# One task for the products with v, and output bias and LayerNorm vectors loaded per group, in a two-layer decoder trunk

## The chip, the cores and the metric

One Trainium2 chip, one of its cores. The metric is the time of the program on the device in microseconds (us); the smaller, the better.

## What is computed

Two layers (DEPTH = 2) run over 2048 rows of 1024 values, all in 32-bit floats. Each layer is one projection into nine pieces, two mixers, a gated sum of the two, an output product and a LayerNorm after the residual sum:

```
h = x @ w_in + b_in                      # q k v z_a u_g v_g z_g g_a g_g
y_a = sliding_window_attention(q, k, v, sinks) * silu(z_a)        # 8 query heads, 2 kv heads, window 128
y_g = spatial_gating(gelu(u_g), gelu(v_g), ...) * silu(z_g)       # LayerNorm(v_g), mixing within chunks of 128 rows
merged = sigmoid(g_a) * (y_a @ w_branch_attn) + sigmoid(g_g) * (y_g @ w_branch_gmlp)
out = merged @ w_out + b_out
x = layer_norm(ALPHA * x + out, ln_g, ln_b)
```

The last two lines use the three vectors of length 1024 that the change is about: `b_out`, `ln_g`, `ln_b`.

## The kernel before

**Groups and units.** Each layer runs over four groups of 512 rows; (l, g) names group g of layer l, so that the order is (0,0), (0,1) ... (1,3). A group works through 54 weight units in order: k, v, four for q, four wide ones for v_g, twelve for z_a, z_g and u_g, sixteen for the gates, eight for the two branch products, and eight (46 to 53) for the output product. A unit is 24 matmuls of 128 x 512 on TensorE (PE), since each product of 32-bit values is made from a high and a low half in three products (`accum_t`, `accum_w`; all of these matmuls are recorded at L178).

**Weights.** In group 0 of a layer a raw unit of 512 KB is loaded to `wr`, split into halves by ScalarE (ACT, L137) and VectorE (DVE, L138), and both halves are stored as `kept` (1 MB). Groups 1 to 3 load the kept halves instead (`w<-kept`, 1 MB, L129). `next_unit` issues the load three or four units ahead. SyncE (SP) issues these loads, those of x and those of the residual, in one queue and in order.

**Side tasks.** Attention, the LayerNorm of v_g, the mixing and the preparing of the next group's x are small tasks in a list (`side`). `mm` calls `step`, which takes a task off the list at a set pace; a scheduler then fixes one order for each engine, and each engine keeps to it. The products with v are `pv_task` (L446): 32 matmuls for each head pair into one bank of PSUM (the accumulators' memory), then a product with `sza` on DVE (L452). In group 0 of a layer there is one task for each pair; in the other six groups there are two, of two pairs each, `pv_task(0, 1)` in the midst of the transposes of the probabilities and `pv_task(2, 3)` after the tasks that normalise v_g.

**The next x.** In groups (0,3), (1,0), (1,1) and (1,2) the next group's x is read from memory, where the LayerNorm left it (`x_later`): eight tiles of 128 x 512, each turned by 16 STREAM_TRANSPOSE instructions on DVE (L291). Those of the first five tiles run in the gate units; those of the last three, 48 instructions, and the splits of these tiles (L203, tiles x) come at the end of the group.

**End of a group.** Eight tiles `y` of residual are loaded (L605) and turned to ALPHA*y + bias on DVE by eight SCALAR_TENSOR_TENSOR (L699). The output product has two halves of 512 columns (h = 0, 1) with four units each; within a unit PE goes over the four row blocks b = 0 to 3, six matmuls each, into four of the five PSUM banks of the pool `MM`. After a half DVE adds each bank to its y (L686) and takes statistics (L688); this is what sets a bank free. The first matmul of h = 1 goes to the fifth bank; that for b = 1 has to wait for the bank that L686 of b = 0, h = 0 empties. The LayerNorm then runs as side tasks in the next group, by ACT (L676) and GpSimd (POOL, L677 and the line behind it).

**The three vectors.** `bo_b`, `lg_b` and `lb_b` are constant tiles of 128 x 1024, each filled by one broadcast DMA of 512 KB from POOL's queue (`out_consts`, L257 to L259), once for each layer: in the first units of (0,0) and around the start of layer 1.

**Temporaries.** `TT` takes a tile of 128 x 512 from the pool `tp`, which has 15.

Of the kernel before, what the change touches and what calls it, by code (L numbers as in the profile page):

```python
# [8 lines left out]
F32 = mybir.dt.float32  # L9
F32R = mybir.dt.float32r  # L10
AF = mybir.ActivationFunctionType
ALU = mybir.AluOpType
PSUM = bass.MemoryType.PSUM

P = 128
# [23 lines left out]
Q_DELAY = 20  # L39
P_DELAY = 10  # L40
LAG = 5
LAG2 = 3
NEARLY = 5


# [5 lines left out]
def trunk_kernel(ctx, tc, xg, xt, wu, bcol, bvg, sinks, lngc, lnb, wsp, bsp, bout, ln_g, ln_b,  # L51
# [4 lines left out]
    def sb(name, bufs):  # L56
        return ctx.enter_context(tc.tile_pool(name=name, bufs=bufs))
# [2 lines left out]
    xp = sb("xp", 2 * KC)  # L60
    yp = sb("yp", 16)
    mp = sb("mp", 16)
    tp = sb("tp", 15)
    wr = sb("wr", 2)
    wp = sb("wp", 4)
    small = sb("small", 3)
# [19 lines left out]
    def TT(shape=None):  # L86
        return tp.tile(shape or [P, T], F32, name=nm("t"), tag="t")
# [4 lines left out]
    def AT(shape=None):  # L92
        return ps_at.tile(shape or [P, T], F32, name=nm("at"), tag="at")

    def S(shape, tag):
        return small.tile(shape, F32, name=nm(tag), tag=tag)
# [119 lines left out]
    vg_b = const.tile([P, GW], F32, name="vg_b")  # L216
    wsT = const.tile([P, NGR, P], F32, name="wsT")
    bias2 = const.tile([P, NGR, P], F32, name="bias2")
    bo_b = const.tile([P, D], F32, name="bo_b")
    lg_b = const.tile([P, D], F32, name="lg_b")  # L220
    lb_b = const.tile([P, D], F32, name="lb_b")
    kept = [[dram.tile([P, 2, 1024], F32, name=f"kept{l}_{n}") for n in range(NUNITS)] for l in range(DEPTH)]
    x1 = [dram.tile([P, NB, D], F32, name=f"x1_{i}") for i in range(NG)]

# [28 lines left out]
                              in0=ps.rearrange("p g t -> p (g t)"), in1=t2, op=ALU.add)  # L253
        return always, go

    def out_consts(l):
        pool.dma_start(out=bo_b, in_=bout[l].partition_broadcast(P))  # L257
        pool.dma_start(out=lg_b, in_=ln_g[l].partition_broadcast(P))
        pool.dma_start(out=lb_b, in_=ln_b[l].partition_broadcast(P))  # L259


    def x_first(g):
# [46 lines left out]
    def group(l, g, xs):  # L309
# [44 lines left out]
            sp.dma_start(out=b8, in_=score_bias)  # L354
            pool.dma_start(out=vg_b, in_=bvg[l].partition_broadcast(P))

        if g == 0 and l > 0:
            out_consts(l)

        sza, szg = [], []  # L360


# [75 lines left out]

        def pv_task(*cs):
            def go():  # L440
                pos = {c: AT() for c in cs}
                for c in cs:
                    for b in range(NB):
                        for kb in range(2):
                            for j in range(2):
                                pe.matmul(pos[c][j * HD:(j + 1) * HD, b * P:(b + 1) * P],  # L446
                                          lhsT=VT[:, b + kb, j * HD:(j + 1) * HD],
                                          rhs=att[c]["p"][b // 2][1 - kb][:, 2 * (b % 2) + j, :],
                                          start=kb == 0, stop=kb == 1, skip_group_check=True)
                for c in cs:  # L450
                    y = TT()
                    dve.tensor_tensor(out=y, in0=pos[c], in1=sza[c], op=ALU.mult)  # L452
                    ys[c] = hilo(Y, y)
                    del att[c]
            return (lambda: count[0] >= due["p", cs[-1], 1]), go
# [28 lines left out]
        for c in range(NPAIR):  # L484
            for hf in range(2):
                for r in range(4):
                    side.append(t_task(c, hf, r))
                    if two and c == 2 and hf * 4 + r == LAG2:
                        side.append(pv_task(0, 1))
                    if not two and c and hf * 4 + r == LAG:  # L490
                        side.append(pv_task(c - 1))
        pace[0] = PACE_T
# [47 lines left out]

        uz = set()
        side.extend([v_stats(b) for b in range(NB)] + [nop] + [v_norm(b) for b in range(NB)])
        side.append(pv_task(2, 3) if two else pv_task(3))
        side.extend(mix_task(gi) for gi in range(NGR))
        for i in range(4):
            ps = item()
# [18 lines left out]
        for c in range(KC):  # L565
            if c == 3 and nl == DEPTH - 1:
                nxt, early, late = x_later(ng)
                pace[0] = PACE_E
                side.extend(early)
            ga = gate(BGA + c)  # L570
            uz.add(4 + c)
            gs[c] = ga, gate(BGG + c)
            if c % 2 == 0:
                continue
            if c == 1:
                flush()
                if l + 1 < DEPTH and g == NG - 1:
                    side.append(mix_consts(l + 1))
                elif l == 0 and g == 0:
                    out_consts(0)  # L580
            for cc in (c - 1, c):
                W = next_unit(P)
                sa, sg = gs.pop(cc)
                pa = MM()
                accum_t(pa, W, 0, ys[0:4])
                dve.tensor_tensor(out=sa, in0=sa, in1=pa, op=ALU.mult)  # L586
                pg = MM()
                accum_t(pg, W, 4, ys[4:8])
                dve.tensor_tensor(out=sg, in0=sg, in1=pg, op=ALU.mult)  # L589
                pool.tensor_tensor(out=sa, in0=sa, in1=sg, op=ALU.add)  # L590
                ms.append(hilo(M, sa))
# [9 lines left out]
        for b in range(NB):  # L601
            for h in range(2):
                row = g * NB + b
                src = xt[row * P:(row + 1) * P] if l == 0 else x1[g][:, b, :]
                sp.dma_start(out=rt[b][h], in_=src[:, h * T:(h + 1) * T])  # L605
        st = S([P, NB, 2, 6], "st2")
        mv = S([P, NB, 2], "mv2")
        rs = S([P, NB, 1], "rs2")
# [21 lines left out]
                               in1=mhalf[:, 0:n].unsqueeze(2), op=ALU.pow)  # L630

        def part(b, h):
            r, hs = rt[b][h], slice(h * T, (h + 1) * T)
            dve.scalar_tensor_tensor(out=r, in0=r, scalar=mv[:, b, 0:1], in1=lg_b[:, hs],
                                     op0=ALU.subtract, op1=ALU.mult)

        def norm(b):
            row = g * NB + b
            dst = out[row * P:(row + 1) * P] if l == DEPTH - 1 else x1[g][:, b, :]
            if last and b == NB - 1:  # L640
                for h in range(2):
                    r, hs = rt[b][h], slice(h * T, (h + 1) * T)
                    if h:
                        part(b, h)
                    dve.scalar_tensor_tensor(out=r, in0=r, scalar=rs[:, b, :], in1=lb_b[:, hs],
                                             op0=ALU.mult, op1=ALU.add)
                    sp.dma_start(out=dst[:, hs], in_=r)
                return
            if last:

                nmr = S([P, 1], "nmr")
                dve.scalar_tensor_tensor(out=nmr, in0=mv[:, b, 0:1], scalar=-1.0, in1=rs[:, b, :],
                                         op0=ALU.mult, op1=ALU.mult)
                own = [(T, D)] if b < NB - 2 else [(0, T), (T, T + 256)]
                rest = (0, T) if b < NB - 2 else (T + 256, D)

                def at(lo, hi):
                    return rt[b][lo // T][:, lo % T:(hi - 1) % T + 1], slice(lo, hi)
                for lo, hi in own:
                    r, cs = at(lo, hi)  # L660
                    dve.scalar_tensor_tensor(out=r, in0=r, scalar=mv[:, b, 0:1], in1=lg_b[:, cs],
                                             op0=ALU.subtract, op1=ALU.mult)
                for lo, hi in own:
                    r, cs = at(lo, hi)
                    dve.scalar_tensor_tensor(out=r, in0=r, scalar=rs[:, b, :], in1=lb_b[:, cs],
                                             op0=ALU.mult, op1=ALU.add)
                r, cs = at(*rest)
                act.activation(out=r, in_=r, func=AF.Identity, bias=nmr, scale=rs[:, b, :])
                pool.tensor_tensor(out=r, in0=r, in1=lg_b[:, cs], op=ALU.mult)
                pool.tensor_tensor(out=r, in0=r, in1=lb_b[:, cs], op=ALU.add)  # L670
                for h in range(2):
                    sp.dma_start(out=dst[:, h * T:(h + 1) * T], in_=rt[b][h])
                return
            for h in range(2):
                r, hs = rt[b][h], slice(h * T, (h + 1) * T)
                act.activation(out=r, in_=r, func=AF.Identity, bias=nm4[:, b, :], scale=rs[:, b, :])  # L676
                pool.tensor_tensor(out=r, in0=r, in1=lg_b[:, hs], op=ALU.mult)  # L677
                pool.tensor_tensor(out=r, in0=r, in1=lb_b[:, hs], op=ALU.add)
                pool.dma_start(out=dst[:, hs], in_=r)

        for h in range(2):
# [12 lines left out]
            for u in range(1 if tail else 4):  # L694
                W = next_unit(T)
                for b in range(NB):
                    accum_w(banks[b], W, ms, u, b)
                    if u == 0:
                        dve.scalar_tensor_tensor(out=rt[b][h], in0=rt[b][h], scalar=ALPHA,  # L699
                                                 in1=bo_b[:, h * T:(h + 1) * T], op0=ALU.mult, op1=ALU.add)  # L700
            if tail:
                Ws = [next_unit(T) for _ in range(3)]
                for b in range(NB):
# [123 lines left out]
```

## Time and profile before

| | us |
|---|---|
| median of 3 runs (2541.79 to 2543.31) | 2541.99 |
| the profiled execution, own time | 2541.27 |
| its span from first to last instruction | 2539.6 |
| PE busy (99% of the span) | 2515.7 |
| DVE busy (57%) | 1438.2 |
| ACT busy (27%) | 692.3 |
| POOL busy (17%) | 427.4 |

The mean granted TensorE clock over the span is 0.998 of its full speed. A timeline has one row for a run of like instructions: start, length, engine, line, operation and tiles, their count, and in brackets the idle time of the engine just before and what ended it. A DMA row ends with the time from issue to landing.

### The profile page before, as it was taken

To read this page: it belongs to the slowest core of one execution; us is meant where nothing else is said; L and a number is where in the kernel's file an instruction comes from. 1 tells how busy PE (TensorE), PEld (TensorE's weight loads), DVE (VectorE), ACT (ScalarE), POOL (GpSimd) and SP (SyncE) were. 2 spreads that over 40 slices of the span, in tenths; PEclk is the share of its full clock that TensorE was granted. 3 is DMA by queue.
4 is the path that set the end of the run, shared out by engine and by line. 5 is a ranking of instruction groups with operands and counts; after the bars stand their busy time and mean duration, and the time that the engine had idled before them with its cause. 6 is when DMAs were issued, how large, how long until landed. Compare 5 with 4: busy or idle time off the path is not lost.

```text
span 2539.6 us, 32405 instructions
## 1 busy us (share of the span) xinstructions
PE 2515.7 (99%) x12176; PEld 2093.2 (82%) x12176; DVE 1438.2 (57%) x3755; ACT 692.3 (27%) x1323; POOL 427.4 (17%) x446
## 2 busy tenths in 40 slices
PE   8999999999999999999999999999999999999998
PEld 6888888888888888888878888888888888888886
DVE  7963568213682137825689577772567724676215
ACT  4433333211431114211154322421115211151110
POOL 1120041100411004210041100420004200032001
PEclk9999999999999999999999999999999999999999
DMA  9788964457554576556776897655665556655454
GB/s 320 252 294 299 325 247 177 167 198 260 205 182 166 198 253 212 181 182 221 252 276 232 293 324 281 220 183 173 224 220 207 181 185 211 225 201 182 176 188 180
DMA packets 116108, 568.39 MB, mean 224 GB/s; under 512 B 12112, under 2 KB 28528, under 8 KB 60528
## 3 DMA queue, kind: packets, MB, share of 16 engines
q1 hardware_dynamic: 109776, 546.35, 61.1%
q0 software_dynamic: 6176, 19.97, 2.1%
q8 instruction: 96, 1.57, 0.2%
q14 instruction: 60, 0.49, 0.1%
HBM read 436.25 MB, written 130.02 MB: 223 GB/s over the span
## 4 chain that ended last, share of the span: by engine, by line
PE 93%; DVE 3%; issue 2%; DMA 1%; ACT 0%; POOL 0%; SPq 0%; DVEq 0%; ACTq 0%; POOLq 0%
PE mm L178 87%; PE at L377 2%; PE at L446 2%; PE at L529 1%; DVE t L291 1%; DMA wr<-in_wu 1%; DVE w L138 0%; DVE y L699 0%; ACT y L676 0%; SPq L267 0%; DVE x L203 0%; POOL rs L629 0%; DVE vt L350 0%; ACT w L137 0%; DVE t L589 0%
## 5 line engine op out<-in xcount | busy, mean ns | idle before, releaser
L178 PE MATMUL mm<-x,w 128*128 128x512 f32 x6528 | 1515.8, 391 | 9.5 <-ACT x L202 7.1
L178 PEld LDWEIGHTS mm<-x,w 128*128 128x128 f32 x6528 | 1220.6, 188 | 265.7 <-ACT x L202 7.6
L178 PE MATMUL mm<-y,w 128*128 128x512 f32 x1536 | 353.6, 389 | 0.0
L178 PE MATMUL mm<-w,m 128*128 128x512 f32 x1536 | 349.8, 389 | 0.2 <-DVE y L686 0.2
L178 PEld LDWEIGHTS mm<-w,m 128*128 128x128 f32 x1536 | 288.3, 188 | 60.4 <-DVE y L686 0.6
L178 PEld LDWEIGHTS mm<-y,w 128*128 128x128 f32 x1536 | 288.3, 188 | 59.8
L427 DVE STREAM_TRANSPOSE t<-t 32x128 f32<-32x128 f32 x1024 | 309.2, 302 | 14.1
L590 POOL TENSOR_TENSOR t<-t,t 128x512 f32<-128x512 f32 x64 | 84.0, 1312 | 1011.3 <-DVE t L589 953.8
L138 DVE TENSOR_TENSOR w<-wr,w 128x1024 fp32r<-128x1024 f32 x108 | 147.7, 1368 | 140.1 <-ACT w L137 139.2
L586 DVE TENSOR_TENSOR t<-t,mm 128x512 f32<-128x512 f32 x64 | 43.7, 683 | 293.0 <-PE mm L178 292.9
L558 ACT ACTIVATE t<-mm,bcol 128x512 f32<-128x512 f32 x128 | 88.2, 689 | 423.2 <-PE mm L178 423.1
L178 PE MATMUL mm<-w,x 128*128 128x512 f32 x768 | 190.7, 392 | 0.0
L291 DVE STREAM_TRANSPOSE t<-t 32x128 f32<-32x128 f32 x512 | 154.9, 303 | 50.7 <-DMA t<-x 43.5
L137 ACT CAST w<-wr 128x1024 fp32r<-128x1024 f32 x108 | 113.1, 1047 | 206.1 <-DMA wr<-in_wu 91.9
L178 PEld LDWEIGHTS mm<-w,x 128*128 128x128 f32 x768 | 139.1, 189 | 25.5
L432 POOL TENSOR_SCALAR_AFFINE_SELECT t<-t 128x512 f32<-128x512 f32 x64 | 44.7, 699 | 572.2 <-DVE t L427 538.2
L202 ACT CAST m<-t 128x512 fp32r<-128x512 f32 x64 | 39.8, 621 | 288.1 <-POOL t L590 288.0
L409 ACT ACTIVATE t<-t,negm 128x128 f32<-128x128 f32 x256 | 99.3, 389 | 55.8 <-DVE negm L399 55.4
L686 DVE TENSOR_TENSOR y<-y,mm 128x512 f32<-128x512 f32 x64 | 43.9, 687 | 119.2 <-PE mm L178 119.2
L385 DVE CUSTOM_DVE_ANT_0 t<-at,b 128x256 f32<-128x256 f32 (+1 forms) x256 | 97.0, 412 | 17.0 <-PE at L377 14.6
L452 DVE TENSOR_TENSOR t<-at,m 128x512 f32<-128x512 f32 x32 | 22.0, 686 | 124.2 <-PE at L446 124.2
L676 ACT ACTIVATE y<-y,nm,rs 128x512 f32<-128x512 f32 x56 | 41.1, 805 | 182.8 <-DVE nm L717 182.6
(104 smaller groups left out, 1780.8 us busy)
## 6 DMA issues: line engine op xcount, KB each, us to landing
w<-kept SPq DMA_DIRECT2D x324, 1024.0 KB, 4.8
kept<-w SPq DMA_DIRECT2D x108, 1024.0 KB, 4.9
wr<-in_wu SPq DMA_DIRECT2D x108, 512.0 KB, 5.9
t<-in_xg SPq DMA_DIRECT2D x32, 256.0 KB, 6.6
y<-in_xt SPq DMA_DIRECT2D x32, 256.0 KB, 6.4
x<-y POOLq DMA_DIRECT2D x32, 256.0 KB, 5.2
t<-x SPq DMA_DIRECT2D x32, 256.0 KB, 5.6
y<-x SPq DMA_DIRECT2D x32, 256.0 KB, 6.3
```

The source lines that it names most:

```text
L137: act.copy(out=t[:, 0, :], in_=r)
L138: dve.tensor_tensor(out=t[:, 1, :], in0=r, in1=f(t)[:, 0, :], op=ALU.subtract)
L178: pe.matmul(o, lhsT=a, rhs=b, start=start, stop=stop, skip_group_check=skip)
L291: dve.transpose(out=outs[k][32 * i:32 * i + 32, :, 32 * r:32 * r + 32], in_=tiles[k][32 * r:32 * r + 32, :, 32 * i:32 * i + 32])
L377: pe.matmul(ps[:, j, :], lhsT=q[c][j][:, b * P:(b + 1) * P], rhs=KT[a][j][:, b * P:b * P + 2 * P], start=a == 0, stop=a == 1)
L385: dve.tensor_tensor_reduce(out=t[:, j, lo:], in0=ps[:, j, lo:], in1=b8[:, 2 * c + j, lo:], scale=1.0, scalar=NEG, op0=ALU.add, op1=ALU.max ...
L409: act.activation(out=w, in_=w, func=AF.Exp, bias=negm[:, bb, j:j + 1], scale=HD ** -0.5, accum_out=sums[:, bb, j:j + 1])
L427: dve.transpose(out=cur_[32 * i:32 * i + 32, :, 32 * r:32 * r + 32], in_=w[32 * r:32 * r + 32, :, 32 * i:32 * i + 32])
L432: pool.affine_select(out=prev_, in_=cur_, pattern=[[0, 4], [-1, P]], compare_op=ALU.is_gt, fill=0.0, base=0, channel_multiplier=1)
L446: pe.matmul(pos[c][j * HD:(j + 1) * HD, b * P:(b + 1) * P], lhsT=VT[:, b + kb, j * HD:(j + 1) * HD], rhs=att[c]["p"][b // 2][1 - kb][:, 2 ...
L558: act.activation(out=t, in_=ps, func=AF.Sigmoid, bias=bias(i))
L590: pool.tensor_tensor(out=sa, in0=sa, in1=sg, op=ALU.add)
```

## The change

`pv_task` takes all four pairs at once in the six groups with g > 0, at the place where pairs 2 and 3 were; its fourth bank comes from the pool `MM`. The constant tiles for the three vectors are gone. Instead `out_consts(l, src)` takes two tiles of 128 x 512 from the temporaries and fills them by two DMAs of 256 KB each from SP's queue; it is called three times in each group, behind the loads of the residual. That is six broadcasts for a group and 48 in all, where six of 512 KB ran in the whole program. The pool of temporaries grows from 15 to 21.

```diff
-    tp = sb("tp", 15)
+    tp = sb("tp", 21)
...
-    bo_b = const.tile([P, D], F32, name="bo_b")
-    lg_b = const.tile([P, D], F32, name="lg_b")
-    lb_b = const.tile([P, D], F32, name="lb_b")
...
-    def out_consts(l):
-        pool.dma_start(out=bo_b, in_=bout[l].partition_broadcast(P))
-        pool.dma_start(out=lg_b, in_=ln_g[l].partition_broadcast(P))
-        pool.dma_start(out=lb_b, in_=ln_b[l].partition_broadcast(P))
+    def out_consts(l, src):
+        ts = [TT() for _ in range(2)]
+        for h in range(2):
+            sp.dma_start(out=ts[h], in_=src[l][h * T:(h + 1) * T].partition_broadcast(P))
+        return ts
...
-        if g == 0 and l > 0:
-            out_consts(l)
...
-                pos = {c: AT() for c in cs}
+                pos = {c: AT() if i < 3 else MM() for i, c in enumerate(cs)}
...
-                    if two and c == 2 and hf * 4 + r == LAG2:
-                        side.append(pv_task(0, 1))
...
-        side.append(pv_task(2, 3) if two else pv_task(3))
+        side.append(pv_task(0, 1, 2, 3) if two else pv_task(3))
...
-                elif l == 0 and g == 0:
-                    out_consts(0)
...
                 sp.dma_start(out=rt[b][h], in_=src[:, h * T:(h + 1) * T])
+        bo_b, lg_b, lb_b = (out_consts(l, src) for src in (bout, ln_g, ln_b))
...
                     if u == 0:
                         dve.scalar_tensor_tensor(out=rt[b][h], in0=rt[b][h], scalar=ALPHA,
-                                                 in1=bo_b[:, h * T:(h + 1) * T], op0=ALU.mult, op1=ALU.add)
+                                                 in1=bo_b[h], op0=ALU.mult, op1=ALU.add)
```

The other uses of the three vectors (LayerNorm) read the new tiles in the same way.

The change moves instructions in two places that matter below. The first is DVE's order at the end of group (0,3). There `t<-t` STREAM_TRANSPOSE are the turns of the next x, `y<-y,bo_b` (after: `y<-y,t`) is ALPHA*y + bias, `t<-t,mm` and `m<-t,m` belong to the last branch products, and `y<-y,mm` empties a bank. Before, the stretch in which the transposes lie and the first three of ALPHA*y + bias:

```order
L291 STREAM_TRANSPOSE t_9798<-t_9342 32x4x32 x14
L586 TENSOR_TENSOR t_9542<-t_9542,mm_9633 128x512
L291 STREAM_TRANSPOSE t_9798<-t_9342 32x4x32 x2
L291 STREAM_TRANSPOSE t_9851<-t_9411 32x4x32 x9
L589 TENSOR_TENSOR t_9571<-t_9571,mm_9647 128x512
L291 STREAM_TRANSPOSE t_9851<-t_9411 32x4x32 x7
L203 TENSOR_TENSOR m_9663<-t_9542,m_9662 128x512
L586 TENSOR_TENSOR t_9600<-t_9600,mm_9668 128x512
L291 STREAM_TRANSPOSE t_9918<-t_9486 32x4x32 x11
L589 TENSOR_TENSOR t_9629<-t_9629,mm_9682 128x512
L699 SCALAR_TENSOR_TENSOR y_9701<-y_9701,bo_b 128x512
```

After, from the fifth ALPHA*y + bias on (the four before it and the last `m<-t,m` lie ahead of these rows, and none of the 48 transposes does):

```order
L691 SCALAR_TENSOR_TENSOR y_9735<-y_9735,t_9747 128x512
L691 SCALAR_TENSOR_TENSOR y_9736<-y_9736,t_9748 128x512
L691 SCALAR_TENSOR_TENSOR y_9737<-y_9737,t_9747 128x512
L288 STREAM_TRANSPOSE t_9838<-t_9370 32x4x32 x16
L288 STREAM_TRANSPOSE t_9891<-t_9439 32x4x32 x16
L288 STREAM_TRANSPOSE t_9957<-t_9514 32x4x32 x8
L691 SCALAR_TENSOR_TENSOR y_9738<-y_9738,t_9748 128x512
L288 STREAM_TRANSPOSE t_9957<-t_9514 32x4x32 x8
L202 TENSOR_TENSOR x_10012<-t_9838,x_10011 128x512
L202 TENSOR_TENSOR x_10030<-t_9891,x_10029 128x512
L202 TENSOR_TENSOR x_10042<-t_9957,x_10041 128x512
L678 TENSOR_TENSOR y_9731<-y_9731,mm_9763 128x512
```

The 48 transposes of the last three tiles lay ahead of the first ALPHA*y + bias but for five; now they all lie behind seven of the eight, between these and the first emptying of a bank. (1,1) and (1,2) read the same. In (1,0) the rows are mixed with the splits of weights: 26 of the 48 lay ahead of the first ALPHA*y + bias and none does now; 36 stand in one run behind the sixth, and five, with the three x splits and one split of weights, have moved behind the first emptying of a bank.

The second place is SP's queue at the end of group (0,1). There `y<-in_xt` are the last loads of the residual and `w<-kept_49` is the weight unit that ends the first half of the output product. Before:

```order
L605 DMA y_4903<-in_xt 128x512
L605 DMA y_4904<-in_xt 128x512
L129 DMA w_4921<-kept_49_158 128x2048
L129 DMA w_4963<-kept_50_159 128x2048
L129 DMA w_5001<-kept_51_160 128x2048
L129 DMA w_5035<-kept_52_161 128x2048
```

After:

```order
L595 DMA y_4909<-in_xt 128x512
L595 DMA y_4910<-in_xt 128x512
L255 DMA t_4919<-in_bout 128x512
L255 DMA t_4920<-in_bout 128x512
L255 DMA t_4923<-in_ln_g 128x512
L255 DMA t_4924<-in_ln_g 128x512
L255 DMA t_4927<-in_ln_b 128x512
L255 DMA t_4928<-in_ln_b 128x512
L128 DMA w_4939<-kept_49_155 128x2048
L128 DMA w_4981<-kept_50_156 128x2048
```

Six broadcasts now stand ahead of unit 49. In (0,2) it is the same; in (0,0) they stand ahead of the raw load of a unit, and in the later groups one to three are ahead of the loads of the residual or among them, and the rest behind.

## Rows read from the trace of the kernel before

**Rows 1.** waits of PE: line, cause, us in total, times, longest

```profile
PE at L377 <- DVE m L467: 3.3, 2, 1.7
PE mm L178 <- DVE w L138: 2.1, 3, 0.8
```

**Rows 2.** PE timeline around products with v, in groups (0,0) and (0,1)

```profile
103.50 1.97 PE L446 MATMUL at<-t,vt 128*64 128x128 f32 x32
105.40 13.44 PE L178 MATMUL mm<-x,w 128*128 128x512 f32 x58
...
427.03 3.71 PE L446 MATMUL at<-t,vt 128*64 128x128 f32 x64
430.67 32.71 PE L178 MATMUL mm<-x,w 128*128 128x512 f32 x143
```

**Rows 3.** timeline of POOL and a DMA view: the start of the program

```profile
12.86 0.54 POOL L257 DMA_DIRECT2D bo_b<-in_bout  x1
...
wr<-in_wu SPq DMA_DIRECT2D x1, 512.0 KB, 11.7
...
wr<-in_wu SPq DMA_DIRECT2D x108, 512.0 KB, 5.9
```

**Rows 4.** SP, DMA, stretch and DVE at the ends of groups (0,1) and (0,2)

```profile
605.74 15.31 SPq L129 DMA_DIRECT2D w<-kept  x5
...
w<-kept SPq DMA_DIRECT2D x1, 1024.0 KB, 7.6
...
604.00:608.00 4.00, 4.00 (x19) 1.00 1.03 371
...
616.65 0.69 DVE L686 TENSOR_TENSOR y<-y,mm 128x512 f32<-128x512 f32 x1 [5.76 <-PE mm L178]
...
917.72 1.12 SPq L129 DMA_DIRECT2D w<-kept  x2
...
w<-kept SPq DMA_DIRECT2D x1, 1024.0 KB, 7.1
...
929.77 0.69 DVE L686 TENSOR_TENSOR y<-y,mm 128x512 f32<-128x512 f32 x1 [6.60 <-PE mm L178]
```

**Rows 5.** DVE timeline at the end of group (0,3)

```profile
1227.07 3.45 DVE L291 STREAM_TRANSPOSE t<-t 32x128 f32<-32x128 f32 x11
1230.55 0.69 DVE L589 TENSOR_TENSOR t<-t,mm 128x512 f32<-128x512 f32 x1
1231.15 2.98 DVE L699 SCALAR_TENSOR_TENSOR y<-y,bo_b 128x512 f32<-128x512 f32 x3
1234.06 0.68 DVE L203 TENSOR_TENSOR m<-t,m 128x512 fp32r<-128x512 f32 x1
1234.66 1.88 DVE L699 SCALAR_TENSOR_TENSOR y<-y,bo_b 128x512 f32<-128x512 f32 x3
...
1239.61 1.90 DVE L203 TENSOR_TENSOR x<-t,x 128x512 fp32r<-128x512 f32 x3
1243.80 0.69 DVE L686 TENSOR_TENSOR y<-y,mm 128x512 f32<-128x512 f32 x1 [2.29 <-PE mm L178]
```

**Rows 6.** PE timeline over the same stretch

```profile
1235.67 20.56 PE L178 MATMUL mm<-w,m 128*128 128x512 f32 x90
```

**Rows 7.** DVE timeline at the end of group (1,2)

```profile
2189.82 0.69 DVE L686 TENSOR_TENSOR y<-y,mm 128x512 f32<-128x512 f32 x1 [2.32 <-PE mm L178]
```

**Rows 8.** DVE and PE timelines at the end of group (1,0)

```profile
1566.80 1.22 DVE L138 TENSOR_TENSOR w<-wr,w 128x1024 fp32r<-128x1024 f32 x1
1567.94 0.68 DVE L686 TENSOR_TENSOR y<-y,mm 128x512 f32<-128x512 f32 x1
...
1568.67 11.64 PE L178 MATMUL mm<-w,m 128*128 128x512 f32 x50 [0.23 <-DVE y L686]
```

**Rows 9.** PE timeline behind the second of two waits at the layer border

```profile
1295.16 0.39 PE L377 MATMUL at<-ka,m 128*128 128x256 f32 x1 [1.56 <-DVE m L467]
...
1295.50 3.80 PE L178 MATMUL mm<-x,w 128*128 128x512 f32 x9
```

More of the change, by code (lines that the diff above doesn't have):

```diff
@@ L41 @@
 LAG = 5
-LAG2 = 3
 NEARLY = 5
@@ L632, in part @@
         def part(b, h):
-            r, hs = rt[b][h], slice(h * T, (h + 1) * T)
-            dve.scalar_tensor_tensor(out=r, in0=r, scalar=mv[:, b, 0:1], in1=lg_b[:, hs],
+            r = rt[b][h]
+            dve.scalar_tensor_tensor(out=r, in0=r, scalar=mv[:, b, 0:1], in1=lg_b[h],
                                      op0=ALU.subtract, op1=ALU.mult)
@@ L644, in norm @@
                         part(b, h)
-                    dve.scalar_tensor_tensor(out=r, in0=r, scalar=rs[:, b, :], in1=lb_b[:, hs],
+                    dve.scalar_tensor_tensor(out=r, in0=r, scalar=rs[:, b, :], in1=lb_b[h],
                                              op0=ALU.mult, op1=ALU.add)
@@ L657, in at @@
                 def at(lo, hi):
-                    return rt[b][lo // T][:, lo % T:(hi - 1) % T + 1], slice(lo, hi)
+                    cs = slice(lo % T, (hi - 1) % T + 1)
+                    return [t[lo // T][:, cs] for t in (rt[b], lg_b, lb_b)]
                 for lo, hi in own:
-                    r, cs = at(lo, hi)
-                    dve.scalar_tensor_tensor(out=r, in0=r, scalar=mv[:, b, 0:1], in1=lg_b[:, cs],
+                    r, lg, _ = at(lo, hi)
+                    dve.scalar_tensor_tensor(out=r, in0=r, scalar=mv[:, b, 0:1], in1=lg,
                                              op0=ALU.subtract, op1=ALU.mult)
                 for lo, hi in own:
-                    r, cs = at(lo, hi)
-                    dve.scalar_tensor_tensor(out=r, in0=r, scalar=rs[:, b, :], in1=lb_b[:, cs],
+                    r, _, lb = at(lo, hi)
+                    dve.scalar_tensor_tensor(out=r, in0=r, scalar=rs[:, b, :], in1=lb,
                                              op0=ALU.mult, op1=ALU.add)
-                r, cs = at(*rest)
+                r, lg, lb = at(*rest)
                 act.activation(out=r, in_=r, func=AF.Identity, bias=nmr, scale=rs[:, b, :])
-                pool.tensor_tensor(out=r, in0=r, in1=lg_b[:, cs], op=ALU.mult)
-                pool.tensor_tensor(out=r, in0=r, in1=lb_b[:, cs], op=ALU.add)
+                pool.tensor_tensor(out=r, in0=r, in1=lg, op=ALU.mult)
+                pool.tensor_tensor(out=r, in0=r, in1=lb, op=ALU.add)
                 for h in range(2):
@@ L676, in norm @@
                 act.activation(out=r, in_=r, func=AF.Identity, bias=nm4[:, b, :], scale=rs[:, b, :])
-                pool.tensor_tensor(out=r, in0=r, in1=lg_b[:, hs], op=ALU.mult)
-                pool.tensor_tensor(out=r, in0=r, in1=lb_b[:, hs], op=ALU.add)
+                pool.tensor_tensor(out=r, in0=r, in1=lg_b[h], op=ALU.mult)
+                pool.tensor_tensor(out=r, in0=r, in1=lb_b[h], op=ALU.add)
                 pool.dma_start(out=dst[:, hs], in_=r)
```

## The prediction

> **What bounds the kernel now.** First the page's busy times: PE works 99% of the span at a granted clock of 0.998, every other engine at most 57%. So only what PE issues, and what it waits for, counts. The waits of PE come second [rows 1]: behind the first matmul there is little, 2.1 us for DVE's splits of weights in the first units and 3.3 us for DVE at the border between the layers. Third I read the timelines where the change moves something: the products with v [rows 2], the start [rows 3], SP and DVE where groups end [rows 4 to 8]. What matters there is how much earlier than PE needs it DVE or a load is done, since there is next to no idle PE time to win, and every new wait is paid in full.
>
> **The products with v.** 64 matmuls of a task with two pairs hold PE from 427.03 to 430.67, 3.64 us; the 32 of a task with one pair from 103.50 to 105.40, 1.90 us [rows 2]. So a pair costs 1.74 us and a task 0.16 us on top. Six tasks go: 6 x 0.16 = **-1.0 us**. A matmul that restarts a little late behind each task could make it -1.6; more waiting of the four pairs for their PSUM banks could make it 0. I take -1.0. DVE empties four banks behind the task instead of two; the mixing tasks that follow use the banks of the same pool, but the main matmuls between them, from another pool, go on, and I cost this at nothing.
>
> **The start.** POOL's three broadcasts, 1.5 MB, begin at 12.86 [rows 3] while raw weights stream in. A raw load issued at 9.55 took 11.7 us to land, where the median of all is 5.9 [rows 3]. PE's 2.1 us of waits for the splits [rows 1] fall in these units. Without the 1.5 MB I expect these waits gone: **-2.1 us**, with 0 as the other end (the loads of x and weights alone may fill the DMA engines).
>
> **The loads at the end of (0,1) and (0,2).** Six broadcasts of 256 KB now stand ahead of weight unit 49 in SP's queue, and their issue waits, as that of unit 49 did, for room behind the loads of the residual. In that stretch the DMA engines are full (share 1.03) and move 371 GB/s [rows 4], so 6 x 0.262 MB take 4.2 us. Unit 49 was issued at 605.74 and landed 7.6 us later, at 613.3. PE needs it when the unit starts: DVE empties bank b = 0 at 616.65, straight after the unit's first six matmuls; six at 20.56/90 = 0.228 us [rows 6] are 1.4 us, and about 0.2 us passes from the last to DVE (an estimate), so it starts at 615.1. There was 1.8 us to spare: **+2.4 us**. In (0,2) it lands at 917.72 + 7.1 = 924.8 and is needed at 929.77 - 1.6 = 928.2: 3.4 to spare, **+0.8 us**. If the broadcasts, all from one small row of memory, move slower than other loads, it is more (+2.8 for a third more time, over both places); if they run beside the others, 0. Behind unit 49 are units 50 and up, in the same queue, with more to spare. In the other groups the loads that are needed soonest stand ahead of most broadcasts, and I take 0. ALPHA*y + bias now has to wait for its vector's broadcast; in (0,1) that ends about 611.4, and eight of them at 0.6 us are done by 616.3, just before DVE may empty b = 0.
>
> **DVE at the end of (0,3), (1,1) and (1,2).** This is the main term. The 48 transposes ran in DVE's gaps ahead of ALPHA*y + bias; the new order has them behind it and right ahead of the emptying of b = 0. The gaps ahead stay empty, since the DVE instructions there wait for PE's branch products: the last `t<-t,mm` cannot begin before 1230.55. From there [rows 5], in the new order and with these rows' durations (start to start):
> - two ALPHA*y + bias (of the three in 2.91 us one is slow), the last `m<-t,m` at about 1234.0, done 1234.6;
> - five ALPHA*y + bias at 0.62: 1237.7;
> - 40 transposes at 3.45/11 = 0.314: 12.5 us, 1250.2; one more ALPHA*y + bias and eight more transposes: 1253.3;
> - three splits of x, 1.85: 1255.2; b = 0 emptied, 0.69: 1255.9.
> The first steps may pass some 0.5 us sooner, so 1255.4 to 1255.9. PE: its last matmul into b = 0 is over at 1243.8 at the latest; 18 matmuls of the other blocks and six for h = 1, b = 0 in the fifth bank follow, 24 x 0.228 = 5.5, so at 1249.3 it wants the bank of b = 0 [rows 5, 6]. It will wait 6.1 to 6.6 us; I take 6.2. The other banks follow at 1.3 us each, PE's own pace. (1,2) has the same 2.3 us of idle DVE ahead of the first emptying [rows 5, 7], and (1,1) reads like it: 3 x 6.2 = **+18.6 us**. The waiting instruction on PE holds back all behind it, and DVE's next work (splits for layer 1, the LayerNorm's statistics) starts as much later as PE does.
>
> The size hangs on what a transpose costs, and here the Trainium skill says something else: "VectorE: DVE Perf Modes", the section on the TRN2 errata, gives 58 cycles and the free size at 0.96 GHz, which would be an estimate of 194 ns for 128 elements. By that the 48 would be done 5.7 us sooner and PE would wait 0.5 us instead of 6.2. The row's 314 ns, in an unbroken run of 11, is what I go by; the same section states that its formula is too low for one instruction and that the measured fixed part is near 150 cycles.
>
> **DVE at the end of (1,0).** Here splits of weights lie between. 26 transposes that ran ahead of the first ALPHA*y + bias now run behind it, 26 x 0.314 = 8.2 us more ahead of the emptying of b = 0; five transposes (1.6), three splits of x (1.9) and a split of weights (1.2 [rows 8]) have gone behind it: 3.4 us later. There is no room at all, since PE already waits 0.23 us for this emptying [rows 8]: **+3.4 us**. It is 2 if DVE comes earlier to the run, and 6 if the split of unit 50, which now lies behind the run as well, and the split that moved between the emptyings add theirs.
>
> **The clock.** At the layer border, behind waits of 1.7 and 1.56 us [rows 1, 9], nine matmuls take 3.80 us instead of 2.05: they went at the lower of the clock's levels. I expect the same behind each of the three waits of 6 us: 3 x 1.75 = **+5.3 us**; 0 and 7 (with (1,0)) are the ends.
>
> **The sum**, on the profiled execution's 2541.3: -1.0 - 2.1 + 2.4 + 0.8 + 18.6 + 3.4 + 5.3 = +27.4, so 2568.7; the median of runs lies 0.7 higher, 2569.4. I say **2569 us**, 1.1% slower.
>
> **Rivals.**
> - The clock stays up behind the waits. For it: gaps under 1 us at the start show no fall. Against it: the border's row. 2569 - 5.3 = 2564.
> - More than summed: the broadcasts are slow, (1,0) costs 6, and the clock falls there too: +2.8, +2.6 and +1.7 on top, 2576; up to 2580 if other loads in the queue come late as well.
> - Part is given back: PE's wait at the layer border (3.3 us and 1.75 for the clock) goes away since PE arrives there later: 2564. Against it: what DVE does there starts later by the same.
> - **Not slower.** The transposes come cheap in a run of 40, so that DVE reaches the bank in time. The deciding point: DVE has to be 6.1 us sooner, 48 transposes at 0.187 us instead of 0.314. Then the three stretches and the clock cost nothing, (1,0) gains 26 x 0.127 = 3.3, all it cost, and 2541.99 - 3.1 + 3.2 = 2542 is left; 2539 if the broadcasts are hidden too. Against it stands every run of transposes in the trace, as in [rows 5]. The rule of the Trainium skill quoted above ("VectorE: DVE Perf Modes") is all but this case: at its 194 ns the time would be some 2544, and I give it 0.02 of this case's chance.
>
> **How the numbers follow.** The main case 0.49; the clock stays up, or the border gives back, 0.20; more than summed 0.14; not slower 0.11; 0.06 for something between, where two of the three stretches are hidden in part (2550). The range leaves out the not-slower case, the one between and the far end of the dear one: 2555 to 2579. About 0.2% (5 us) is what a measurement of this kernel can tell from no change. Within it lies the not-slower case; faster by more, 2537 or less, would need it with all gains at their best ends and the border's wait gone as well. I give that 0.03 of the 0.11. So faster 0.03, same 0.08, slower 0.89.
>
> **What would show it.** In the waits of PE a new entry at the output product for DVE's emptying of a bank, four times, the longest above 6 us, beside runs of 40 transposes in DVE's timeline at 1237 to 1250 (shifted); matmuls at 0.427 us behind them; a wait of 2 us for `w<-kept` near 615; the waits for L138 at the start gone. The forecast is wrong if the transposes run ahead of ALPHA*y + bias or at under 0.2 us each, if PE has another free bank for b = 1, or if DVE is done with its part before 1249.

## The result, and the profile after

The changed kernel takes 2556.17 us (median of 4 runs, 2555.49 to 2557.97), the one before 2541.89 in the runs beside it: 1.0057 times as long, 95% interval 1.0046 to 1.0069. The forecast was 2569, range 2555 to 2579. The direction was right; the loss of 14.3 us is about half of the 27 foreseen.

The page's line of PE, then the waits of PE in the changed kernel (columns as in [rows 1]):

```profile
PE 2519.5 (99%) x12176; PEld 2096.5 (82%) x12176; DVE 1438.6 (56%) x3755; ACT 697.6 (27%) x1327; POOL 425.1 (17%) x440
```

```profile
PE mm L177 <- DVE y L678: 7.2, 4, 2.2
PE mm L177 <- ACT x L201: 6.7, 2, 6.4
PE mm L177 <- DMA w<-kept: 4.5, 2, 2.9
PE at L371 <- DVE m L461: 3.7, 2, 2.2
PE mm L177 <- DVE w L137: 0.8, 1, 0.8
```

The wait for ACT (L201) lies at the start and stands in the kernel before too (7.1 us). Two entries are new: four waits for DVE's emptying of a bank (L678), 7.2 us, and two for weight units, 4.5 us. The waits for splits at the start (L137) are down from 2.1 to 0.8 [rows 1]. Since both kernels issue the same 10368 main matmuls in one order, they can be set side by side number by number; what a stretch gained or lost, by the start times of its matmuls in the two profiled runs, is then

| where | foreseen | measured |
|---|---|---|
| start, up to the z units of (0,0) | -2.1 | -2.6 |
| products with v, six groups | -1.0 | -2.3 (6 x -0.38) |
| unit 49 in (0,1) | +2.4 | +4.7 |
| unit 49 in (0,2) | +0.8 | +1.9 |
| second half of the output product: (0,3), (1,1), (1,2) | +23.9 (18.6, and 5.3 for the clock) | +2.5, +4.1, +4.1 |
| the same in (1,0) | +3.4 | +1.2 |
| layer border | 0 | +0.5 |
| sum | +27.4 | +14.1 |

DVE at the end of (0,3), which answers to [rows 5]:

```profile
1226.48 0.69 DVE L202 TENSOR_TENSOR m<-t,m 128x512 fp32r<-128x512 f32 x1 [2.06 <-ACT m L201]
1227.09 0.68 DVE L576 TENSOR_TENSOR t<-t,mm 128x512 f32<-128x512 f32 x1
1229.17 0.69 DVE L579 TENSOR_TENSOR t<-t,mm 128x512 f32<-128x512 f32 x1 [1.41 <-PE mm L177]
1230.16 2.22 DVE L691 SCALAR_TENSOR_TENSOR y<-y,t 128x512 f32<-128x512 f32 x2 [0.30 <-DMA y<-in_xt]
1232.30 0.68 DVE L202 TENSOR_TENSOR m<-t,m 128x512 fp32r<-128x512 f32 x1
1232.90 3.09 DVE L691 SCALAR_TENSOR_TENSOR y<-y,t 128x512 f32<-128x512 f32 x5
1235.91 12.66 DVE L288 STREAM_TRANSPOSE t<-t 32x128 f32<-32x128 f32 x40
1248.59 0.69 DVE L691 SCALAR_TENSOR_TENSOR y<-y,t 128x512 f32<-128x512 f32 x1
1249.30 2.52 DVE L288 STREAM_TRANSPOSE t<-t 32x128 f32<-32x128 f32 x8
1251.85 1.90 DVE L202 TENSOR_TENSOR x<-t,x 128x512 fp32r<-128x512 f32 x3
1253.66 0.68 DVE L678 TENSOR_TENSOR y<-y,mm 128x512 f32<-128x512 f32 x1
```

and PE over the same stretch, which answers to [rows 6]:

```profile
1237.81 14.44 PE L177 MATMUL mm<-w,m 128*128 128x512 f32 x63
1254.40 7.82 PE L177 MATMUL mm<-w,m 128*128 128x512 f32 x33 [2.14 <-DVE y L678]
```

The order is the forecast one: five ALPHA*y + bias, 40 transposes in one run of 12.66 us, 0.316 each, one more, eight more, three splits of x, then the emptying; and PE waits for it. But it waits 2.14 us, not 6.2. The row that decides is 1229.17: the last product with an accumulator (L579, L589 before) starts there behind 1.41 us of idle time that PE ended. PE's matmuls are 3.1 us later here than in the kernel before, so against them this product starts 4.5 us sooner than at the 1230.55 of [rows 5]. There it stood right behind eleven transposes, with no idle time ahead of it.

The products with v in group (0,1), which answer to [rows 2]:

```profile
455.45 5.46 PE L440 MATMUL at<-t,vt 128*64 128x128 f32 x96
460.74 1.92 PE L440 MATMUL mm<-t,vt 128*64 128x128 f32 x32
462.59 1.88 PE L177 MATMUL mm<-x,w 128*128 128x512 f32 x7
```

128 matmuls hold PE for 7.14 us; the two tasks before took twice 3.64. With the gap behind, a merged task gains 0.38 us.

### The profile page after: what moved, and what is told of

Same layout as the page of the kernel before. It is cut to its first block, busy times and chain, and to the rows that moved or that the text cites. A ratio compares the mean times of both kernels' runs of the same rounds, so it can differ in the third digit from the quotient of the medians.

```text
span 2553.8 us, 32516 instructions
## 1 busy us (share of the span) xinstructions
PE 2519.5 (99%) x12176; PEld 2096.5 (82%) x12176; DVE 1438.6 (56%) x3755; ACT 697.6 (27%) x1327; POOL 425.1 (17%) x440
## 4 chain that ended last, share of the span: by engine, by line
PE 89%; issue 4%; DVE 3%; DMA 3%; ACT 0%; POOL 0%; SPq 0%; DVEq 0%; POOLq 0%; ACTq 0%
PE mm L177 83%; PE at L371 2%; PE at L440 2%; DVE t L288 2%; DMA t<-in_xg 1%; PE at L521 1%; DMA y<-x 1%; DMA w<-kept 1%; DMA y<-in_xt 0%; DVE y L691 0%; PE mm L440 0%; DMA wr<-in_wu 0%; DVE w L137 0%; ACT y L668 0%; DVE x L202 0%
## 5 line engine op out<-in xcount | busy, mean ns | idle before, releaser
L177 PE MATMUL mm<-w,m 128*128 128x512 f32 x1536 | 356.6, 393 | 11.8 <-DVE y L678 7.2
L137 DVE TENSOR_TENSOR w<-wr,w 128x1024 fp32r<-128x1024 f32 x108 | 148.6, 1376 | 133.8 <-ACT w L136 132.9
L576 DVE TENSOR_TENSOR t<-t,mm 128x512 f32<-128x512 f32 x64 | 43.7, 682 | 313.3 <-PE mm L177 313.3
L201 ACT CAST m<-t 128x512 fp32r<-128x512 f32 x64 | 39.8, 621 | 286.8 <-POOL t L580 286.8
L379 DVE CUSTOM_DVE_ANT_0 t<-at,b 128x256 f32<-128x256 f32 (+1 forms) x256 | 97.7, 413 | 18.6 <-PE at L371 16.6
L678 DVE TENSOR_TENSOR y<-y,mm 128x512 f32<-128x512 f32 x64 | 43.7, 684 | 100.3 <-PE mm L177 100.3
L493 ACT ACTIVATE m<-mm,bcol 128x512 f32<-128x512 f32 x64 | 44.1, 689 | 180.0 <-PE mm L177 179.9
L579 DVE TENSOR_TENSOR t<-t,mm 128x512 f32<-128x512 f32 x64 | 44.0, 687 | 82.9 <-PE mm L177 82.7
```

The source lines that it names most:

```text
L137: dve.tensor_tensor(out=t[:, 1, :], in0=r, in1=f(t)[:, 0, :], op=ALU.subtract)
L177: pe.matmul(o, lhsT=a, rhs=b, start=start, stop=stop, skip_group_check=skip)
L379: dve.tensor_tensor_reduce(out=t[:, j, lo:], in0=ps[:, j, lo:], in1=b8[:, 2 * c + j, lo:], scale=1.0, scalar=NEG, op0=ALU.add, op1=ALU.max ...
```

## Experiments

Each was timed in turn with the kernel before on the same chip. The median of the kernel before was 2541.5 to 2542.0 wherever it ran more than once, so medians of different experiments are set side by side too. (0,1) and the like name groups as above.

### The merge alone (e1)

The edit, to the kernel before (the line that adds the task of the first two pairs goes as well):

```diff
-                pos = {c: AT() for c in cs}
+                pos = {c: AT() if i < 3 else MM() for i, c in enumerate(cs)}
...
-        side.append(pv_task(2, 3) if two else pv_task(3))
+        side.append(pv_task(0, 1, 2, 3) if two else pv_task(3))
```

> The kernel before with the four pairs in one task and nothing else. Theory (the merge saves its fixed cost, 0.3 us in each of six groups by the shifts of matmuls between the two traces, and moves no transpose): -1.8 us, 2540. Rival (the merge is what makes the scheduler move the transposes, or its four banks make DVE late): +5 us or more, with waits of PE for DVE's emptying of a bank at the output product.

Measured: 2547.27 against 2542.03, ratio 1.0022 (1.0013 to 1.0031). So the merge alone is a loss of 5 us, as the rival had it in size, though for neither reason. Its waits of PE, and a piece of PE's and of POOL's timeline at the end of the task in (0,1):

```profile
PE mm L446 <- POOL t L432: 2.8, 6, 0.5
...
PE mm L446 <- POOL t L434: 1.6, 6, 0.3
```

```profile
462.81 1.04 PE L446 MATMUL mm<-t,vt 128*64 128x128 f32 x16
464.32 0.44 PE L446 MATMUL mm<-t,vt 128*64 128x128 f32 x4 [0.47 <-POOL t L432]
465.03 0.88 PE L446 MATMUL mm<-t,vt 128*64 128x128 f32 x12 [0.27 <-POOL t L434]
```

```profile
463.63 0.64 POOL L432 TENSOR_SCALAR_AFFINE_SELECT t<-t 128x512 f32<-128x512 f32 x1 [1.59 <-DVE t L427]
464.34 0.64 POOL L434 TENSOR_SCALAR_AFFINE_SELECT t<-t 128x512 f32<-128x512 f32 x1
```

The last quarter of the task waits for POOL's two masks of the last pair (L432, L434), and the first of these waited for DVE's transposes. The four pairs need 16 tiles of probabilities at once (four each), and this kernel has 15 temporaries; e9, below, shows that this is the cause. Each of the six groups loses 0.8 us where the changed kernel gains 0.38. That would make 4.9 us, and the whole shift of the profiled run is 5.0.

### The loads per group alone (e2)

To the changed kernel:

```diff
+                    if two and c == 2 and hf * 4 + r == LAG2:
+                        side.append(pv_task(0, 1))
...
-        side.append(pv_task(0, 1, 2, 3) if two else pv_task(3))
+        side.append(pv_task(2, 3) if two else pv_task(3))
```

> The changed kernel with the two tasks of two pairs put back, so that the loads per group and the larger pool are what is left of the change. Theory (all of the loss comes with the loads): 2556.2 + 1.8 = 2558, with the same waits for L678's instruction (about 7 us in four) and for weight units (about 4.5 us in two). Rival (the loss needs the merge): 2542 or so.

Measured: 2557.33, ratio 1.0064 (1.0048 to 1.0080). The waits of the profiled run, which at 2551.85 was the fastest of its four:

```profile
PE mm L179 <- DVE y L682: 7.7, 4, 2.2
...
PE mm L179 <- DMA w<-kept: 2.4, 2, 1.4
```

All of the loss comes with the loads, and so does the new order on DVE: it is the same here as in the changed kernel. In e3, below, where two tiles instead of six are taken from the temporaries ahead of the late transposes, 26 of the 48 come back ahead. By what reckoning the scheduler moves them is not shown. That the profiled run is 5.5 us under the median has a visible part in the clock: behind the three waits of 2.2 us at the ends of (0,3), (1,1) and (1,2) the granted clock stayed at 1.00, while in the changed kernel's profile it fell behind two of them.

### Sixteen transposes fewer (e7)

To `x_later` of the changed kernel:

```diff
-                res[k] = hilo(X, outs[k].rearrange("p b t -> p (b t)"))
+                res[k] = hilo(X, outs[min(k, KC - 2)].rearrange("p b t -> p (b t)"))
...
-            (early if k < NEARLY else late).extend(mk_turn(k, r) for r in range(4))
+            (early if k < NEARLY else late).extend(mk_turn(k, r) for r in range(4) if k < KC - 1)
```

> The changed kernel with the last tile of the next x not turned where x comes from memory (the tile before it is used twice): 16 of the 48 late transposes are left out, and the other 32 stay behind ALPHA*y + bias. Theory (PE waits at the output product for DVE's chain, transpose for transpose): DVE reaches the emptying 16 x 0.314 = 5.0 us sooner, more than the 2.2 us of each wait; the waits and the falls of the clock behind them go, 2544. Rival (PE waits for the first emptying since its matmuls or the loads are late): 2554 to 2556.

Measured: 2544.40, ratio to the kernel before 1.0008 (0.9998 to 1.0017): 12 us less than the changed kernel. The runs spread from 2539.98 to 2547.50, and the profiled one is the slowest of the ten. Its DVE at the end of (0,3), where PE is 6.6 us later than in the kernel before:

```profile
1232.71 0.69 DVE L579 TENSOR_TENSOR t<-t,mm 128x512 f32<-128x512 f32 x1 [1.41 <-PE mm L177]
...
1239.46 10.12 DVE L288 STREAM_TRANSPOSE t<-t 32x128 f32<-32x128 f32 x32
...
1252.03 0.68 DVE L678 TENSOR_TENSOR y<-y,mm 128x512 f32<-128x512 f32 x1
```

In all four groups no wait for L678 is left, and the stretch of the second half loses nothing in (0,3), (1,1) and (1,2). So the run of transposes ahead of the emptying is what PE waited for. The waits for weight units stayed (5.2 us in two, 2.9 and 2.3), and in this run the clock fell behind both.

### What held the last product back in the kernel before (e8)

The same edit in the kernel before.

> The kernel before with the same 16 transposes left out, which leaves none between the second-last and the last product with an accumulator (L589) at the end of (0,3). It is for one row: when does that last product begin, which began at 1230.55 in the kernel before? Theory (it was held back by the transposes ahead of it on DVE, not by PE): about 4 us sooner against PE's matmuls, with an idle DVE ahead of it that PE ends. The prediction's reading (PE's accumulator is not done before): unmoved, at 1230.5 against the same matmuls. The time does not move in either case: 2542.

Measured: 2541.23 in one run. The rows:

```profile
1227.15 0.68 DVE L586 TENSOR_TENSOR t<-t,mm 128x512 f32<-128x512 f32 x1
1227.75 1.89 DVE L203 TENSOR_TENSOR x<-t,x 128x512 fp32r<-128x512 f32 x3
1229.56 0.68 DVE L589 TENSOR_TENSOR t<-t,mm 128x512 f32<-128x512 f32 x1
```

PE is 0.7 us later here than in the kernel before, so the product, at 1229.56, starts 1.7 us sooner against it: neither 4 us with idle time ahead, nor unmoved. The three splits of x (L203, 1.89 us) have moved ahead of it and hold it now. It does show that PE's accumulator was done before 1230.55; how much sooner DVE can have it is shown by the changed kernel, where it waited for it, idle for 1.41 us.

### LayerNorm vectors loaded later: in four groups (e6), in two (e5), in all (e3)

To the changed kernel. `late_c` is true in e6 where the next x is read from memory, in e5 in (0,1) and (0,2), in e3 always:

```diff
-        bo_b, lg_b, lb_b = (out_consts(l, src) for src in (bout, ln_g, ln_b))
+        bo_b = out_consts(l, bout)
+        lg_b, lb_b = (None, None) if late_c else (out_consts(l, src) for src in (ln_g, ln_b))
...
             tail = last and h == 1
+            if h == 1 and late_c:
+                lg_b, lb_b = (out_consts(l, src) for src in (ln_g, ln_b))
```

> The changed kernel, with the loads of the two LayerNorm vectors behind the first half of the output product in (0,3) to (1,2) alone, where 26 of the 48 transposes lie ahead of ALPHA*y + bias again. Theory (DVE's order costs 2.5 + 1.2 + 4.1 + 4.1 us there by the shift of matmuls, clock falls with it): waits for L678 gone, those for weight units stay; 2556.2 - 11.9 = 2544. Rival (PE waits there for something else that is late too): 2552 or more.

> The changed kernel, with the loads of the two LayerNorm vectors behind the first half of the output product in groups (0,1) and (0,2) alone; DVE's order at the ends of (0,3) to (1,2) stays that of the changed kernel. Theory (the bytes of six broadcasts ahead of weight unit 49 make its 4.5 us of waits and the fall of the clock behind the longer of the two; two broadcasts fit in its room of 1.8 us): the waits for weight units go, those for L678 stay at about 7 us; 2556.2 - 4.6 - 1.9 = 2550. Rival (the residual's loads or ALPHA*y + bias are what is late there): 2556.

> The changed kernel, but in every group the loads of the two LayerNorm vectors are issued behind the first half of the output product; only the two tiles of the output bias are loaded ahead. By its order 26 of the 48 transposes lie ahead of ALPHA*y + bias again, and two broadcasts instead of six lie ahead of weight unit 49. Theory (the DVE order and the bytes ahead of unit 49 are the two causes): both kinds of PE waits go, and 2541.9 - 2.3 for the start - 1.8 for the merge = 2538 is left. Rival (broadcasts on SP's queue cost by themselves, wherever they stand): 2548 or more.

Measured: e6 2541.83, ratio 1.0005 (0.9995 to 1.0014); e5 2552.05, 1.0034 (1.0020 to 1.0048); e3 2538.45, 0.9984 (0.9975 to 0.9993). The new waits of PE, for e6, e5 and e3 in turn:

```profile
PE mm L177 <- DMA w<-kept: 2.9, 2, 1.8
```

```profile
PE mm L177 <- DVE y L680: 7.5, 4, 2.3
```

```profile
PE mm L177 <- ACT x L201: 7.6, 2, 6.4
PE at L371 <- DVE m L461: 3.7, 2, 2.2
PE mm L177 <- DVE w L137: 0.3, 1, 0.3
```

Each edit takes away its own kind of wait and leaves the other, and with both only those of the kernel before are left. Against the changed kernel e5 gains 4.1 us, e6 14.3 and e3, with both, 17.7: the two causes add up. e6 came out 2 us under what was foreseen and e5 2 us over it, which is within the spread of their runs (2540.36 to 2544.73, and 2547.10 to 2552.64). In e3 DVE empties the first bank at the end of (0,3) with time to spare again:

```profile
1234.41 1.29 DVE L202 TENSOR_TENSOR x<-t,x 128x512 fp32r<-128x512 f32 x2
1235.62 2.82 DVE L288 STREAM_TRANSPOSE t<-t 32x128 f32<-32x128 f32 x9
1240.78 0.69 DVE L680 TENSOR_TENSOR y<-y,mm 128x512 f32<-128x512 f32 x1 [2.35 <-PE mm L177]
```

e3 is the version to keep: faster than the kernel before by 0.16%, where the changed kernel is slower by 0.57%.

### Parts of the gain (e4, e9, e10)

e4 is the kernel before with the merge, and its three broadcasts of layer 0 held back:

```diff
+                    pool.tensor_copy(out=bo_b[:, 0:1], in_=ga[:, 0:1])
+                    pool.tensor_copy(out=lg_b[:, 0:1], in_=ga[:, 0:1])
+                    pool.tensor_copy(out=lb_b[:, 0:1], in_=ga[:, 0:1])
                     out_consts(0)
```

> The kernel before with the merge, and with the three broadcasts of layer 0 held back until the second gate unit of the first group (one column of each tile is first written from a gate tile); constant tiles and POOL's queue as before. Theory (both gains of the change can be had without its loads per group): -1.8 - 2.1 = 2538, 0.15% under the kernel before. Rival (the start is bound by the loads of x and weights alone): 2540, as the merge alone.

Measured: 2545.80, ratio 1.0015 (1.0006 to 1.0024). Not what was expected, since the merge costs 5 us here as in e1; against e1 it is 1.5 us less, which bears out the start.

e9 is e3 with `sb("tp", 15)`:

> The kernel of e3 (merge, loads per group, those of the LayerNorm vectors late) with 15 temporaries instead of 21. Theory (one task for four pairs needs 16 tiles of probabilities at once; with 15 the masks of the last pair on POOL come behind a product with L541 and PE waits for them, as in e1, where each of six groups lost 0.8 us instead of gaining 0.4): waits of PE for POOL at the products with v return, 2538.5 + 6 x 1.2 = 2545.6. Rival (the loss in e1 came from the constant tiles or POOL's queue): 2538.5.

Measured: 2543.80, 1.0009 (1.0000 to 1.0018): 5.4 us over e3, with the same two waits for POOL as e1 (2.8 and 1.6 us). So it is the number of temporaries.

e10 is e3 with the two tasks of two pairs:

> The kernel of e3 with the two tasks of two pairs put back. Theory (with room for its tiles the merge is worth 0.38 us in each of six groups): 2538.5 + 2.3 = 2540.8. Rival (the merge is worth nothing, all of e3's gain is the start): 2538.5.

Measured: 2539.32, 0.9990 (0.9981 to 0.9999). The difference to e3, 0.9 us, is less than the 2.3 foreseen and within the spread of both. In the profiled runs the six merges gain their 6 x 0.38, and the start of e3 gains 1.8 us more than that of e10; at the layer border e3 loses 1.7 us that e10 does not. That is the clock: over the same 12 us there (PE busy, granted clock, DMA share, GB/s; e3, then e10) it was granted 0.72 and 0.86, and 0.14 of 12 us are 1.7.

```profile
1290.00:1302.00 12.00, 10.39 (x38) 0.72 0.85 310
1290.00:1302.00 12.00, 8.76 (x36) 0.86 0.85 328
```

Why it stayed low for longer in e3 is not shown.

### Broadcasts against loads of the same size (e11)

To the changed kernel:

```diff
-            sp.dma_start(out=ts[h], in_=src[l][h * T:(h + 1) * T].partition_broadcast(P))
+            sp.dma_start(out=ts[h], in_=xt[0:P, h * T:(h + 1) * T])
```

> The changed kernel, but the six tiles of each group are filled from 128 rows of x instead of one row repeated for all partitions: same bytes, same queue, same places in every order; the output bias and the LayerNorm vectors are left out of the result by that. Theory (a broadcast moves slower than a load of the same size: at the end of (0,1) the changed kernel moved 265 to 287 GB/s where the kernel before moved 371): with own rows the stretch goes back to about 370 GB/s, and PE waits for unit 49 about 2.2 us in (0,1) and 0.6 to 0.8 in (0,2), as the prediction's sum had it, instead of 2.9 and 1.6. Rival (the stretch is slow for another reason, such as the order of landing): waits as in the changed kernel.

One run, 2554.97. The stretch at the end of (0,1): PE's busy time, granted clock, DMA share and GB/s, first in the changed kernel, then here:

```profile
604.00:608.00 4.00, 4.00 (x19) 1.00 0.99 265
608.00:612.00 4.00, 4.00 (x19) 1.00 1.03 287
```

```profile
604.00:608.00 4.00, 4.00 (x20) 1.00 1.00 348
608.00:612.00 4.00, 4.00 (x19) 1.00 1.07 407
```

```profile
PE mm L177 <- DMA w<-kept: 1.9, 2, 1.4
```

348 and 407 GB/s instead of 265 and 287, at the same share of busy DMA engines, and waits of 1.4 and 0.6 us for unit 49 instead of 2.9 and 1.6. The traces of e2, e6 and e7, which have the same six broadcasts there, tell how far this holds. In e2:

```profile
604.00:608.00 4.00, 4.00 (x19) 1.00 1.10 378
608.00:612.00 4.00, 4.00 (x20) 1.00 1.00 279
```

e6 moved 335 and 308, e7 357 and 239. Over the eight microseconds the four kernels with broadcasts moved 276 (the changed kernel) to 329 GB/s (e2), against 378 in e11 and 367 in the kernel before. From the issue of the first of the six to the landing of unit 49 they took 12.0 to 13.0 us, e11 11.6; in (0,2) 11.6 to 12.3, e11 11.2. So six broadcasts cost some 0.4 to 1.4 us more than six plain loads there, with one execution of the plain ones to go by. The wait of PE shows less of it: for unit 49 in (0,1) e2 waited 1.35 us, as long as e11.

## Why the prediction was right, and where its sizes were wrong

**What bounds the kernel, and the direction: right.** PE has no spare time, the change hides nothing that PE waited for except at the start, and two new waits stand in the waits of PE, at the places named. e5, e6 and e3 show them to be independent and together the whole loss.

**DVE at the ends of (0,3), (1,1), (1,2): the mechanism right, the size wrong by half, +10.7 instead of +23.9.** The failed step is "the last `t<-t,mm` cannot begin before 1230.55". Its row [rows 5] stands directly behind a run of transposes and carries no bracket of idle time: DVE was busy, so that start was DVE's, not PE's. When the transposes left, it started 4.5 us sooner against PE. The rest of the chain was right: from this product to the end of the emptying it took 25.2 us, 25.4 in the prediction. By its end at 1255.9 the wait was 6.6 (6.2 was taken), and 6.6 - 4.5 leaves 2.1; the waits were 2.1 to 2.2. In (1,0) the last product began 3.6 us sooner against PE as well, and the stretch lost 1.2 us instead of 3.4; the prediction had "2 if DVE comes earlier to the run". The price of a transpose was right (0.316 in a run of 40, foreseen 0.314): the 194 ns estimated from the Trainium skill's formula ("VectorE: DVE Perf Modes", the section on the TRN2 errata) do not hold for it. What that section of the Trainium skill says of its own formula, a measured fixed part near 150 cycles instead of 58, comes closer: it makes an estimate of 290 ns for 128 elements.

**The clock: 5.3 us foreseen, about that much found, in part elsewhere.** It fell behind unit 49 in (0,1) and at the ends of (1,1) and (1,2), and not in (0,3). Those three stretches lost 1.8 to 1.9 us more than their waits, (0,3) 0.3 more, so a fall costs some 1.6 us (1.75 foreseen). The waits of 6 us for which it was foreseen never came; that three falls came all the same, one of them at a place where none was foreseen, is luck.

**Unit 49: right place, too small.** +4.7 instead of +2.4 in (0,1): 2.9 us of wait, and 1.8 behind it, most of that the clock, which the sum put at nothing here. In (0,2) it is +1.9 instead of +0.8, 1.6 of it the wait. Unit 49 was issued at 606.31 and landed 8.9 us later, 615.2; PE started it at 615.37:

```profile
w<-kept SPq DMA_DIRECT2D x1, 1024.0 KB, 8.9
```

```profile
615.37 24.95 PE L177 MATMUL mm<-w,m 128*128 128x512 f32 x102 [2.89 <-DMA w<-kept]
```

The mis-sized term of the wait is 6 x 0.262 MB at 371 GB/s. The stretch moved 265 to 287 in this execution (e11 above), which would make 5.5 to 5.9 us instead of 4.2 and a wait of 3.7 to 4.1 instead of 2.4: more than the 2.9 found, so the sum by GB/s is rough. The prediction had slower broadcasts as a bound, and took the faster end.

**The merge: -2.3 instead of -1.0,** the gap behind each task included, which was the bound of -1.6 and a little more. What was missed altogether is that the larger pool is no by-part of the change: without it the merge costs 5 us (e1, e9).

**The start: -2.1 foreseen, -2.6 in this profile.** The stretch is not steady: among the kernels without the early broadcasts it gained 3.3 us in the profile of e9 and lost 1.0 in that of e5.

**The rivals, and the range.** "The clock stays up" came true in part, and so did the slow broadcasts of "more than summed"; "not slower" did not. In kind the result is nearest to "something between", stretches hidden in part (2550), which the range left out. That the time lies inside the range, 1.2 us above its lower end, is in part luck: the forecast had no case between 2550 and 2564.

## What to carry to other kernels

Before taking a start time from a trace as the earliest possible, look at what stands ahead of it on its engine: only a row with idle time ahead, ended by another engine, tells when its input was ready. Work that fills gaps ahead of a chain is free there and behind it costs what the chain has no room for (here 15 us of transposes cost waits of 2.1 to 2.2 us), so read in the new order where it went. And parts of one change may carry one another: here the constants' room paid for the temporaries that the merge needs, and loading the vectors in two steps (e3) keeps the gains without the new waits.

## What the runs showed of the hardware that was not expected

Waits of the same length were sometimes followed by a fall of the TensorE clock and sometimes not. In one execution of the changed kernel PE waited 2.14 us in (0,3) and 2.15 us in (1,2); the four microseconds behind each (PE busy, granted clock, DMA share, GB/s):

```profile
1254.00:1258.00 4.00, 3.60 (x16) 1.00 0.27 111
2209.00:2213.00 4.00, 4.00 (x13) 0.57 0.00 0
```

At 0.57 the matmuls ran mostly at 1.2 GHz instead of 2.4. In e11 the clock fell in (0,3) too, behind 2.3 us; in the profiled run of e2 behind none of the three. With the fall that stretch lost 4.2 us, without it 2.5. Such falls are much of the spread between runs of these kernels: the fastest run of e2, 2551.85, has a mean granted clock of 0.998, the slowest, 2560.09, one of 0.995, and 0.003 of 2556 us are 7.7 (an estimate from the two). And DMA engines with a full busy share can move a quarter less: 265 GB/s at a share of 0.99 with broadcasts among the loads, 371 at 1.03 without [rows 4]; how much less varied from run to run (279 to 378 in e2, at 1.00 and 1.10).
